# A trunk of six modulated sub-layers on one core: its opening in two parts of 512 features, with the modulation's sums in PSUM and two issuing queues

## The chip, the cores and the metric

One core of a Trainium2 chip runs the whole program, once per execution. The metric is the device time of one execution in microseconds (us), the median of three. Shorter is better.

## What is computed

The reference takes 256 rows of 1024 features through two layers of three sub-layers each. Every sub-layer computes, with `cs = silu(c)`,

```python
mod = (cs @ mod_w[layer] + mod_b[layer]).reshape(bsz, N_SUB, 3, D_MODEL)
shift, scale, gate = m[:, None, 0], m[:, None, 1], m[:, None, 2]
y = f(x * (1 + scale) + shift)
return layer_norm(DEEPNORM_ALPHA * x + (1 + gate) * y, ln_g, ln_b)
```

For the first, third, fourth and sixth sub-layer `f` is a SwiGLU, `0.5 * (silu(u @ w_gate) * (u @ w_up)) @ w_down`, with 2816 inner features; the second is a sparse attention beside a gated DeltaNet, the fifth a latent attention. All data are float32. `mod_w` has 1024 rows and, for each sub-layer, three parts of 1024 columns: shift (part 0), scale (part 1) and gate (part 2).

## The kernel before

Features lie on the 128 partitions, so a vector of 1024 features is 8 columns of 128. A product in near float32 precision is made of three TensorE passes: each operand is split into a rounded high part (ScalarE, the CAST of line 258) and the rest (the subtraction of line 259, on VectorE or GpSimd, called "low part" here). `u`, the modulated input, is kept as `uT`, features by rows, in both parts.

The modulation vectors come from `mod_gen` (line 185). It loads `mod_w` in pieces of 128 rows, and VectorE adds `w * c_k` into a 128x1024 sum in SBUF, one SCALAR_TENSOR_TENSOR per piece (line 225; the first of a sum is the TENSOR_SCALAR of line 218). TensorE then adds over the partitions: with matmuls against a column of ones for the first sub-layer (`mod_cols0`, line 142, matmul at 147), with a matmul against a matrix of ones for a gate (`mod_gate`, lines 180 and 182). `mod_gen` is a Python generator; `pace` draws from it while the SwiGLU runs, so that the eight gate rows of the first sub-layer are summed during its chunks.

The opening is everything up to the first SwiGLU product. All loads go through SyncE's queue: the four scale DMAs and the first three of shift (two pieces each, 1 MB, rows of 4 KB; the tag `w8` has three buffers), with `x` behind the scale, then the last two pieces of shift and the first two column blocks of gate and up weights. VectorE sums all 1024 features of scale, then of shift. `make_u` (line 269) with both row blocks turns `x` into `acc` banks (line 282), applies scale and shift to 256 features at a time (lines 296 on VectorE and 298 on ScalarE) and splits the result. The SwiGLU then walks 11 chunks of 256 inner features: `load` (line 439) fetches 1 MB of gate and 1 MB of up weights, TensorE makes 96 products of 128x256 (chunk 0 in the order of the list at line 495, line 540; the others through `mm3`, lines 263 to 265), and each chunk is followed by the down products of the chunk before (24 of 128x512, `down`, with weights from `load_down`, line 456). Down weights share three buffers of the tag `wd` with the gate rows of `mod_w`; the low part of the first eight down tiles is made on GpSimd.

`setup_rest` hands out small set-up work (masks, positions) between chunks. The order on each engine is set by a list scheduler that has its own cost model; `behind(...)` only forces one instruction after another on its engine. SyncE's queue issues in order: a DMA that waits, for a free buffer or for an earlier DMA on the same one of eight completion lanes (DMAHW0 to DMAHW7), holds all that stand behind it.

`warm` issues an idle TensorE product; nothing reads it.

## Time and profile before

| | us |
|---|---|
| median of 3 runs | 1210.27 (1207.26 to 1211.66) |
| the profiled execution | 1209.47 |
| its span, first to last instruction | 1207.7 |
| first SwiGLU product starts | 31.93 |
| last of chunk 1's gate and up products done, first down product | 58.02 |

Times of day below count from the span's start. The span is 1.8 us shorter than the execution that it comes from, and that execution is 0.8 us below the median. A timeline row gives start and length, the engine, the line of the kernel, the operation, and what it writes and reads (output<-inputs); in brackets is the idle time before it and what ended that. Matmul lengths overlap each other, so the distance between starts tells more than a length. A buffer's number is left out of names.

### The profile page before, as it was taken

To read this page: it belongs to the slowest core of one execution; us is meant where nothing else is said; L and a number is where in the kernel's file an instruction comes from. 1 tells how busy PE (TensorE), PEld (TensorE's weight loads), DVE (VectorE), ACT (ScalarE), POOL (GpSimd) and SP (SyncE) were. 2 spreads that over 40 slices of the span, in tenths; PEclk is the share of its full clock that TensorE was granted. 3 is DMA by queue.
4 is the path that set the end of the run, shared out by engine and by line. 5 is a ranking of instruction groups with operands and counts; after the bars stand their busy time and mean duration, and the time that the engine had idled before them with its cause. 6 is when DMAs were issued, how large, how long until landed. Compare 5 with 4: busy or idle time off the path is not lost.

```text
span 1207.7 us, 19560 instructions
## 1 busy us (share of the span) xinstructions
PE 1131.0 (94%) x7703; PEld 1025.9 (85%) x7703; DVE 917.7 (76%) x1404; ACT 548.5 (45%) x963; POOL 259.4 (21%) x186
## 2 busy tenths in 40 slices
PE   4998999998899998999999999999989998999997
PEld 3887999788787887989999899898988877899995
DVE  6699777698986677878775889767789748866545
ACT  0645444456433445543543543434347656544430
POOL 0631000224731452320000342000122234300001
PEclk9998999999999999999999899999989999999999
DMA  9879998453310576789987488888733335885620
GB/s 354 266 252 342 299 327 299 139 179 119 97 36 5 188 270 218 238 293 320 311 298 248 134 284 283 270 278 298 250 122 102 139 105 190 294 253 185 211 71 35
DMA packets 155333, 259.74 MB, mean 215 GB/s; under 512 B 8813, under 2 KB 117354, under 8 KB 155242
## 3 DMA queue, kind: packets, MB, share of 16 engines
q1 hardware_dynamic: 155050, 258.45, 64.4%
q8 instruction: 60, 0.98, 0.3%
q14 instruction: 31, 0.25, 0.1%
q10 hardware_dynamic: 192, 0.05, 0.0%
HBM read 257.43 MB, written 1.05 MB: 214 GB/s over the span
## 4 chain that ended last, share of the span: by engine, by line
PE 51%; DVE 23%; DMA 13%; issue 5%; ACT 4%; POOL 3%; SPq 0%; POOLq 0%; DVEq 0%; ACTq 0%
PE gu L265 8%; PE gu L263 8%; PE gu L264 8%; PE acc L265 6%; PE acc L264 6%; PE acc L263 6%; DMA wd<-ffn_w_down 5%; DMA wd<-mod_w 4%; DVE macc L225 3%; DMA w<-ffn_w_up 2%; DVE g L259 2%; DVE x L383 1%; POOL hd L259 1%; DMA w<-mod_w 1%; DVE u L259 1%
## 5 line engine op out<-in xcount | busy, mean ns | idle before, releaser
L225 DVE SCALAR_TENSOR_TENSOR macc<-wd,csT,macc 128x1024 f32<-128x1024 f32 x112 | 171.5, 1531 | 28.6 <-DMA wd<-mod_w 28.0
L265 PE MATMUL gu<-uT,g 128*128 128x256 f32 x640 | 181.3, 283 | 1.6 <-DVE g L259 1.6
L263 PE MATMUL gu<-uT,g 128*128 128x256 f32 x640 | 181.2, 283 | 1.3 <-ACT sg L548 1.3
L265 PE MATMUL gu<-uT,u 128*128 128x256 f32 x640 | 181.3, 283 | 1.0 <-DVE u L259 1.0
L263 PE MATMUL gu<-uT,u 128*128 128x256 f32 x640 | 181.2, 283 | 0.0
L264 PE MATMUL gu<-uT,u 128*128 128x256 f32 x640 | 181.1, 283 | 0.0
L264 PE MATMUL gu<-uT,g 128*128 128x256 f32 x640 | 181.1, 283 | 0.0
L258 ACT CAST hd<-wd 128x1024 fp32r<-128x1024 f32 x88 | 92.3, 1049 | 136.8 <-DMA wd<-ffn_w_down 118.8
L263 PE MATMUL acc<-hd,h 128*128 128x512 f32 x352 | 141.5, 402 | 0.5 <-ACT h L258 0.5
L265 PE MATMUL acc<-hd,h 128*128 128x512 f32 x352 | 138.0, 392 | 1.8 <-DVE h L259 1.8
L264 PE MATMUL acc<-hd,h 128*128 128x512 f32 x352 | 138.1, 392 | 0.0
L259 DVE TENSOR_TENSOR g<-w,g 128x1024 fp32r<-128x1024 f32 x86 | 117.0, 1364 | 23.9 <-ACT g L258 23.8
L263 PEld LDWEIGHTS gu<-uT,g 128*128 128x128 f32 x640 | 122.7, 192 | 3.2 <-ACT sg L548 1.8
L265 PEld LDWEIGHTS gu<-uT,g 128*128 128x128 f32 x640 | 122.7, 192 | 2.2 <-DVE g L259 2.2
L264 PEld LDWEIGHTS gu<-uT,g 128*128 128x128 f32 x640 | 122.7, 192 | 1.4
L265 PEld LDWEIGHTS gu<-uT,u 128*128 128x128 f32 x640 | 122.9, 192 | 1.2 <-DVE u L259 1.2
L264 PEld LDWEIGHTS gu<-uT,u 128*128 128x128 f32 x640 | 122.9, 192 | 0.0
L263 PEld LDWEIGHTS gu<-uT,u 128*128 128x128 f32 x640 | 122.9, 192 | 0.0
L259 DVE TENSOR_TENSOR u<-w,u 128x1024 fp32r<-128x1024 f32 x81 | 106.6, 1321 | 20.1 <-ACT u L258 20.0
L259 POOL TENSOR_TENSOR hd<-wd,hd 128x1024 fp32r<-128x1024 f32 x32 | 89.6, 2806 | 137.9 <-ACT hd L258 137.9
L258 ACT CAST u<-w 128x1024 fp32r<-128x1024 f32 (+1 forms) x89 | 91.7, 1038 | 58.1 <-DMA w<-ffn_w_up 44.8
L259 POOL TENSOR_TENSOR hl<-w,hl 128x1024 fp32r<-128x1024 f32 x28 | 72.5, 2602 | 202.0 <-ACT hl L258 201.5
(403 smaller groups left out, 2477.6 us busy)
## 6 DMA issues: line engine op xcount, KB each, us to landing
wd<-mod_w SPq DMA_DIRECT2D x130, 512.0 KB, 4.8
wd<-ffn_w_down SPq DMA_DIRECT2D x88, 512.0 KB, 4.6
w<-ffn_w_gate SPq DMA_DIRECT2D x43, 1024.0 KB, 8.4
w<-ffn_w_up SPq DMA_DIRECT2D x43, 1024.0 KB, 6.3
w<-hyb_w_in SPq DMA_DIRECT2D x16, 1024.0 KB, 6.1
w<-mod_w SPq DMA_DIRECT2D x7, 1024.0 KB, 7.5
w<-hyb_w_out SPq DMA_DIRECT2D x4, 1024.0 KB, 5.0
w<-mla_w_out SPq DMA_DIRECT2D x4, 1024.0 KB, 5.1
```

The lines of the kernel that those rows point to most:

```text
L225: step = nc.vector.scalar_tensor_tensor(acc, w, c, acc, ALU.mult, ALU.add)
L258: i = self.nc.scalar.copy(hi, src)
L259: return i, (eng or self.nc.vector).tensor_tensor(out=lo, in0=src, in1=hi.bitcast(F32), op=ALU.subtract)
L263: nc.tensor.matmul(out, lh, rh, start=first, stop=False)
L264: nc.tensor.matmul(out, lh, rl, start=False, stop=False)
L265: self.last_mm = nc.tensor.matmul(out, ll, rh, start=False, stop=last)
L383: V.tensor_tensor(out=x[:, b, sl], in0=tmp, in1=x[:, b, sl], op=ALU.add)
```

## The change

The first sub-layer's scale and shift leave `mod_gen`; `opening`, called from `ffn`, makes them in two halves of 512 features. For each half `open` loads scale (two pieces of 128x4x512, rows of 2 KB), then shift, and adds them in a PSUM bank; only the last addition writes SBUF. `x` comes in two halves and the first half (features 0 to 511) of the weights of chunks 0 and 1 with it, issued by ScalarE (`early`, `load(c, 0)`); the second half of these weights goes through SyncE. GpSimd makes the low parts of six of the eight weight pieces (128x1024 each), VectorE of two. TensorE makes chunk 0's products of the first half (48), then, after the second half's scale is summed over partitions and `x` is turned, chunk 1's (48), and then the second halves of both. One `warm` call of six idle products follows the first turn of `x`, one of two stands ahead of the second halves.

```diff
+    def open(self, hf, after, first, second):
+
+
+        nc, t = self.nc, self.t
+        cols, ks = slice(hf * 512, hf * 512 + 512), slice(4 * hf, 4 * hf + 4)
+        A, B = self.AB[0]
+        for i in (1, 0):
+            acc, pt = self.open_acc[i][:, cols], self.bank("gu")
+            for q in range(2):
+                if i and not q:
+                    first()
+                r = self.tl(self.wp, [P, 4, 512], "w8", bufs=3)
+                src = t["mod_w"][0, q * 512 : (q + 1) * 512, i * D + hf * 512 : i * D + hf * 512 + 512]
+                nc.sync.dma_start(r, src.rearrange("(q p) f -> p q f", p=P))
+                for k in range(4):
+                    c = self.cs[:, 4 * q + k : 4 * q + k + 1]
+                    if q or k:
+                        nc.vector.scalar_tensor_tensor(acc if q and k == 3 else pt, r[:, k], c, pt, ALU.mult, ALU.add)
+                    else:
+                        nc.vector.tensor_scalar_mul(pt, r[:, k], c)
+            if not i:
+                second()
+            pt = pt[:, 0:4]
+            with self.behind(*after):
+                for k in range(4):
+                    nc.tensor.matmul(pt[:, k : k + 1], acc[:, k * P : (k + 1) * P], self.one[:, 0:1], start=True, stop=True)
+            if i:
+                nc.vector.scalar_tensor_tensor(A[:, ks], pt, 1.0, self.bcol[:, 0, 1, ks], ALU.add, ALU.add)
+                turned = []
+                for k0 in range(4 * hf, 4 * hf + 4, 2):
+                    px = self.bank("acc", (P, 2, S))
+                    turned.append((k0, px))
+                    with self.behind(*after):
+                        for q in range(2):
+                            for b in range(NB):
+                                nc.tensor.transpose(px[:, q, b * P : (b + 1) * P],
+                                                    self.x[:, b, (k0 + q) * P : (k0 + q + 1) * P], self.ident)
+                if not hf:
+                    self.warm(self.x[:, 0, 0:512], 6)
             else:
...
+                nc.vector.tensor_tensor(out=B[:, ks], in0=pt, in1=self.bcol[:, 0, 0, ks], op=ALU.add)
+        for k0, px in turned:
+            v = self.tl(self.wp, [P, 2, S], "tmp", bufs=2)
+            nc.vector.tensor_scalar(v[:, 0], px[:, 0], A[:, k0 : k0 + 1], B[:, k0 : k0 + 1], ALU.mult, ALU.add)
+            nc.scalar.activation(v[:, 1], px[:, 1], AF.Identity, scale=A[:, k0 + 1 : k0 + 2], bias=B[:, k0 + 1 : k0 + 2])
+            self.marks[1:] = self.split(self.u[:, 0, k0 : k0 + 2], self.u[:, 1, k0 : k0 + 2], v)
...
+    def opening(self, wg, wu, gp):
+
+
+        nc, t = self.nc, self.t
+        self.x = self.tl(self.wp, [P, NB, D], "x")
+        self.open_acc = [self.tl(self.wp, [P, D], "G", bufs=2) for _ in range(2)]
+        self.AB[0] = [self.tl(self.const, [P, KD], n, bufs=3) for n in "AB"]
+        self.u = u = self.tl(self.wp, [P, 2, KD, S], "uT", F32R)
+        hls, pts, seen = {}, {}, []
+
+        def load(c, hf):
+            if hf:
+                both = self.tl(self.wp, [P, 2, 4, 256], "w8", bufs=3)
+            for g, w in enumerate((wg, wu)):
+                r = both[:, g] if hf else self.tl(self.wp, [P, 4, 256], "wd", bufs=3)
+                src = w[hf * 512 : hf * 512 + 512, c * 256 : (c + 1) * 256]
+                (nc.sync if hf else nc.scalar).dma_start(r, src.rearrange("(k p) f -> p k f", p=P))
+                hls[c, hf, g] = hl = self.tl(gp, [P, 2, 4, 256], "gu"[g], F32R)
+                seen[:] = self.split(hl[:, 0], hl[:, 1], r, None if hf and not g else nc.gpsimd)[:1]
+
+        def early(hf):
+            cols = slice(hf * 512, hf * 512 + 512)
+            with self.behind(*seen):
+                nc.scalar.dma_start(self.x[:, :, cols], t["x"][0][:, cols].rearrange("(b p) d -> p b d", p=P))
+            with self.behind(*seen):
+                load(hf, 0)
+
+        def products(c, hf):
+            if not hf:
+                pts[c] = [self.bank("gu" if c else "acc", (P, 2, S)) for _ in range(2)]
+            for kp in (0, 2):
+                for q in range(3):
+                    for s in range(2):
+                        for g in range(2):
+                            for k in (kp, kp + 1):
+                                self.last_mm = nc.tensor.matmul(
+                                    pts[c][s][:, g], hls[c, hf, g][:, q // 2, k, s * P : (s + 1) * P], u[:, q % 2, 4 * hf + k],
+                                    start=not (hf or k or q or g), stop=hf == 1 and q == 2 and k == 3, skip_group_check=True)
+
+        self.setup_bias()
+        self.open(0, (), lambda: early(0), lambda: None)
+        products(0, 0)
+        self.open(1, (self.last_mm,), lambda: early(1), lambda: [load(0, 1), load(1, 1)])
+        products(1, 0)
+        with self.behind(self.last_mm):
+            self.warm(self.x[:, 0, 0:512], 2)
+
+        def rest(c):
+            products(c, 1)
+            return {(s, g): pts[c][s][:, g] for s in range(2) for g in range(2)}
+
+        return rest
```

In `mod_gen` the list begins with the gate, and `ffn` and `run` take the new path:

```diff
-        todo = [(si, i, k) for si in range(len(self.subs)) for i in (1, 0, 2) for k in range(KD)]
-        ws, loaded, G, step = {}, 0, None, None
+        todo = [(si, i, k) for si in range(len(self.subs)) for i in (1, 0, 2) for k in range(KD) if si or i == 2]
+        ws, loaded, G = {}, 0, None
...
-                        yield
+                ahead = None
+                part = self.opening(wg, wu, gp)
...
             for c in range(NC):
                 tok = c == 0 and ahead is not None
                 with self.behind(*self.marks if c == 1 and ahead else hm.get(c - 2, ())):
-                    if c or ahead:
+                    if c > 1 or ahead:
                         hls = ahead if tok else load(c, False)
                 if tok:
                     rows = by_rows(hls)
                 else:
-                    pts = {(s, g): self.bank("gu", (P, S)) for s in r2 for g in r2}
-                    if c:
+                    if c < 2 and not ahead:
+                        pts = part(c)
+                    else:
+                        pts = {(s, g): self.bank("gu", (P, S)) for s in r2 for g in r2}
...
-        self.lead = 0
+        self.lead, self.count = 0, 2 * KD
+        self.AB, self.G, self.mdone = {}, {}, {(0, 0), (0, 1)}
...
-        self.need(0, 1)
-        self.count += next(self.bg)
-        todo = self.todo = [self.sublayer(si, l, j) for si, (l, j) in enumerate(subs)]
-        self.make_u(0, self.x, range(NB))
+        todo = [self.sublayer(si, l, j) for si, (l, j) in enumerate(subs)]
```

`warm` issues `n` products into one bank, and `mod_cols0`, `load_x`, the joint branch of `make_u` and the interleaving order of chunk 0 are gone.

How the instructions now stand, at three places. Names end in a buffer number; what is in square brackets is what the instruction waits for.

**SyncE's queue at the start.** `w` is a piece of the modulation weights, `prow` the small parameter loads of the set-up, `wd` a down weight tile. Before:

```order
L202 DMA w_5_82<-mod_w 128x2x1024
L202 DMA w_6_86<-mod_w 128x2x1024
L202 DMA w_7_90<-mod_w 128x2x1024 [waits DMAHW1_49]
L202 DMA w_8_94<-mod_w 128x2x1024 [waits DMAHW2_49,DVE_49]
L325 DMA x_118<-x 128x2x1024 [waits DMAHW3_49]
L202 DMA w_14_121<-mod_w 128x2x1024 [waits DMAHW4_49,DVE_49]
L202 DMA w_22_149<-mod_w 128x2x1024 [waits DMAHW5_49,DMAHW1_49,DVE_49]
L202 DMA w_23_153<-mod_w 128x2x1024 [waits DMAHW6_49,DMAHW2_49,DVE_49]
```

Now:

```order
L266 DMA w_19_116<-mod_w 128x4x512
L266 DMA w_20_122<-mod_w 128x4x512
L266 DMA w_25_151<-mod_w 128x4x512
L100 DMA prow<-ln_g 48x128 [waits DMAHW5_49,DVE_49]
L101 DMA prow<-ln_b 48x128 [waits DMAHW6_49]
L102 DMA prow<-mla_q_norm_g 3x128 [waits DMAHW7_49]
L103 DMA prow<-mla_kv_norm_g 2x128 [waits DMAHW1_49]
L483 DMA wd_420<-ffn_w_down 128x1024 [waits DMAHW4_49,Pool_49]
L266 DMA w_26_157<-mod_w 128x4x512 [waits DMAHW5_49,DMAHW2_49,DVE_49]
L266 DMA w_36_240<-mod_w 128x4x512 [waits DMAHW6_49,DVE_49]
L266 DMA w_37_246<-mod_w 128x4x512 [waits DMAHW7_49,DVE_49]
```

Of the eight modulation pieces three are issued at once. The fourth (w_26, the second piece of the first half's shift) stands behind `prow`, whose third load waits on lane 7, that of w_25, and behind down tile 0 (wd_420), which waits for GpSimd: its buffer is the one that chunk 0's first up piece leaves when its low part is made.

**VectorE at the start, now.** gu_104 is the bank of the scale's sum, gu_150 that of the shift's, both of the first half.

```order
L81 COPY csT<-gu_77 128x8 [waits PE_49]
L272 TENSOR_SCALAR gu_104<-w_19_116,csT 128x512 [waits DMAHW2_49,DVE_49]
L272 TENSOR_SCALAR gu_150<-w_25_151,csT 128x512 [waits DMAHW7_49]
L270 SCALAR_TENSOR_TENSOR gu_104<-w_19_116,csT,gu_104 128x512 [waits DVE_49]
L270 SCALAR_TENSOR_TENSOR gu_150<-w_25_151,csT,gu_150 128x512 [waits DVE_49]
```

The alternation goes on through the four 128x512 parts of w_19 and of w_25, then come the four of w_20, and the four of w_26 behind them. So the second addition of scale stands behind the first of shift, which waits for w_25 (lane 7). Before, one sum was finished before the other began.

**SyncE's queue in the first chunks.** `G` rows are the gate's rows of `mod_w` (line 182 now, 198 before). Before:

```order
L458 DMA wd_489<-ffn_w_down 128x1024 [waits DVE_49]
L458 DMA wd_500<-ffn_w_down 128x1024 [waits DMAHW5_49,DMAHW2_49,Pool_49]
L212 DMA G_506<-mod_b 128x1024
L198 DMA wd_508<-mod_w 128x1024 [waits DMAHW6_49,DMAHW4_49,Pool_49]
L198 DMA wd_511<-mod_w 128x1024 [waits DMAHW1_49,Pool_49]
```

Now:

```order
L467 DMA w_80_559<-ffn_w_gate 128x8x256 [waits DMAHW1_49,DVE_49]
L467 DMA w_81_560<-ffn_w_up 128x8x256 [waits DMAHW4_49,DMAHW2_49,DMAHW5_49,DVE_49,Pool_49]
L483 DMA wd_503<-ffn_w_down 128x1024 [waits DMAHW3_49,Pool_49]
L182 DMA wd_511<-mod_w 128x1024 [waits Pool_49]
L182 DMA wd_514<-mod_w 128x1024 [waits Pool_49]
L467 DMA w_102_782<-ffn_w_gate 128x8x256 [waits DMAHW7_49,DMAHW6_49,DVE_49]
L483 DMA wd_681<-ffn_w_down 128x1024 [waits DMAHW3_49,Pool_49]
```

Before, down tiles 2 and 3 and the first gate row went out ahead of chunk 2's weights; now chunk 2's weights are ahead, and down tile 3 (wd_503) and the first two gate rows each wait for GpSimd to finish a down tile's low part.

## Rows read from the trace of the kernel before

**Rows 1.** The page, busy time of TensorE, share of the span, instructions.
```profile
PE 1131.0 (94%) x7703; PEld 1025.9 (85%) x7703; DVE 917.7 (76%) x1404; ACT 548.5 (45%) x963; POOL 259.4 (21%) x186
```

**Rows 2.** Stages of the span, TensorE: length, busy (records), granted clock, DMA share, GB/s.
```profile
32.00:44.00 12.00, 12.00 (x94) 1.00 0.90 292
44.00:58.00 14.00, 12.81 (x105) 1.00 0.64 223
58.00:93.00 35.00, 33.62 (x237) 1.00 0.78 262
93.00:103.00 10.00, 5.82 (x16) 0.66 1.04 358
103.00:230.00 127.00, 127.00 (x887) 1.00 0.85 287
```

**Rows 3.** Timeline of TensorE, 46 to 104 us: start, length, operation, idle before.
```profile
46.61 0.39 PE L265 MATMUL gu<-uT,g 128*128 128x256 f32 x1 [1.19 <-DVE g L259]
...
58.02 0.48 PE L265 MATMUL acc<-hd,h 128*128 128x512 f32 x1
...
97.92 3.75 PE L180 MATMUL gu<-macc,one 128*128 128x512 f32 x4 [4.18 <-DVE macc L225]
100.69 1.41 PE L263 MATMUL acc<-hd,h 128*128 128x512 f32 x1
...
102.98 0.39 PE L264 MATMUL acc<-hd,h 128*128 128x512 f32 x1
```

**Rows 4.** Waits of TensorE from 32 to 230 us: total, times, longest.
```profile
PE gu L180 <- DVE macc L225: 4.2, 1, 4.2
```

**Rows 5.** One line of TensorE by its source: ns min/median/max of one.
```profile
L180 PE MATMUL gu<-macc,one x24: 590/592/1191, 97.9 to 1184.6; 128*128 128x512 f32 x24
```

**Rows 6.** The DMA view of 0 to 45 us: GB/s in 40 equal slices.
```profile
GB/s 0 11 153 408 415 418 412 383 408 390 390 426 411 411 419 408 408 411 408 419 404 415 411 329 291 289 290 290 290 329 401 394 353 349 213 22 110 365 378 387
```

**Rows 7.** Timeline of VectorE in the opening, the same columns.
```profile
6.22 0.75 DVE L218 TENSOR_SCALAR G<-w,csT 128x1024 f32<-128x1024 f32 x1 [3.19 <-DMA w<-mod_w]
...
9.05 7.91 DVE L225 SCALAR_TENSOR_TENSOR G<-w,csT,G 128x1024 f32<-128x1024 f32 x6 [0.76 <-DMA w<-mod_w]
```

**Rows 8.** Groups by form, the down weights on ScalarE and GpSimd.
```profile
L258 ACT CAST hd<-wd 128x1024 fp32r<-128x1024 f32 x88 | 92.3, 1049 | 136.8 <-DMA wd<-ffn_w_down 118.8 <-PE acc L265 10.9 <-POOL poscr L622 6.8
...
L259 POOL TENSOR_TENSOR hd<-wd,hd 128x1024 fp32r<-128x1024 f32 x32 | 89.6, 2806 | 137.9 <-ACT hd L258 137.9
```

**Rows 9.** Groups by form, VectorE: shapes, count, busy us, mean ns, idle before.
```profile
L225 DVE SCALAR_TENSOR_TENSOR macc<-wd,csT,macc 128x1024 f32<-128x1024 f32 x112 | 171.5, 1531 | 28.6 <-DMA wd<-mod_w 28.0
...
L381 DVE SCALAR_TENSOR_TENSOR tmp<-acc,G 128x512 f32<-128x512 f32 x18 | 12.0, 678 | 6.8 <-PE acc L265 6.8
```

**Rows 10.** Timeline of TensorE in the opening, the same columns.
```profile
26.71 1.96 PE L124 MATMUL gu<-x,ident 128*128 128x512 f32 x4
28.75 1.92 PE L147 MATMUL gu<-one,G 128*128 128x1 f32 x16
...
31.93 0.80 PE L540 MATMUL gu<-uT,g 128*128 128x256 f32 x2
```

**Rows 11.** Timeline of ScalarE in the opening.
```profile
30.52 0.56 ACT L298 ACTIVATE tmp<-acc,B,A 128x256 f32<-128x256 f32 x1 [0.46 <-DVE B L168]
31.12 0.62 ACT L258 CAST uT<-tmp 128x512 fp32r<-128x512 f32 x1
```

**Rows 12.** DMA issues by line: KB each, median us to landing.
```profile
wd<-mod_w SPq DMA_DIRECT2D x130, 512.0 KB, 4.8
```

**Rows 13.** Timeline of VectorE, the position operations and the last gate row.
```profile
90.99 0.28 DVE L618 TENSOR_SCALAR posc<-posi 128x258 int32<-128x258 int32 x1
...
96.50 1.28 DVE L225 SCALAR_TENSOR_TENSOR macc<-wd,csT,macc 128x1024 f32<-128x1024 f32 x1
```

**Rows 14.** Timeline of GpSimd and of VectorE around 78 us.
```profile
77.16 3.04 POOL L259 TENSOR_TENSOR hd<-wd,hd 128x1024 fp32r<-128x1024 f32 x1 [6.99 <-ACT hd L258]
...
77.87 3.42 DVE L225 SCALAR_TENSOR_TENSOR macc<-wd,csT,macc 128x1024 f32<-128x1024 f32 x1
```

More of the change, by code (lines that the diff above doesn't have):

```diff
@@ L239, in mod_sums @@
         elif i == 1:
-            if si:
-                self.mod_scale(si, self.mod_cols(acc))
-            else:
-                self.scale = self.mod_cols0(acc, self.one[:, 0:1])
-        else:
-            if not si:
-                with self.behind(step):
-                    self.mod_scale(si, self.scale)
-                    self.nc.vector.tensor_tensor(out=self.AB[0][1], in0=self.share[:, 0:KD], in1=self.bcol[:, 0, 0],
-                                                 op=ALU.add)
+            self.mod_scale(si, self.mod_cols(acc))
+        else:
             self.mod_shift(si, acc)
@@ L301, in make_u @@
-        if joint:
-            pts = [rows(k0) for k0 in range(0, KD, 2)]
-            vs = self.tl(self.wp, [P, 2, 2, W], "macc")
-            self.warm(n[:, 0, 0:512])
-            while self.count < 2 * KD:
-                self.count += next(self.bg)
-            next(self.todo[0])
-            self.need(si, 0)
-            with self.behind(self.last_col):
-                for _ in range(2):
-                    self.warm(n[:, 0, 0:512])
-            for k0 in range(0, KD, 2):
-                with self.behind(self.marks[1]):
-                    affine(k0, pts[k0 // 2])
-                if k0 < 4:
-                    with self.behind(self.marks[1]):
-                        self.marks[1:] = self.between[k0 // 2]()
-        else:
-            for k0 in range(0, KD, 2):
-                affine(k0, rows(k0))
@@ L558, in ffn @@
                         load_down(i)
-                    with self.behind(*[part] if c == 1 else after):
+                    with self.behind(*[made] if c == 1 else after):
                         self.pace(max(0, i + 1 - skip) / (NT - 2 - skip))
@@ L562, in ffn @@
                 if c > 1 and self.left is not None:
-                    with self.behind(part):
+                    with self.behind(made):
                         next(self.left, None)
```

135 lines of the change are left out of this document (32 added, 103 removed).

## The prediction

> **What bounds the kernel now.** I read the page first: TensorE is busy 1131.0 us, 94% of the span [rows 1]. So I looked for the stretches in which it is not, and cut the span into stages [rows 2]. From 103 to 230 us it has 127.00 us of records in 127: whatever delay reaches that stage comes out at the end one for one, since every engine's order is the old one from there on. Lost time lies ahead of it: all of 0 to 31.93, 1.19 in the stage 44 to 58 [rows 3], 1.38 (35.00 - 33.62) in 58 to 93, and 4.18 before the gate's product at line 180 (97.92), which waited for the last gate row's sum (TensorE's waits, [rows 4]). In that last stage the granted clock is 0.66, in all others 1.00. The 1.19 us wait at 46.61 left its stage at 1.00; the 4.18 did not.
>
> What the 4.18 cost besides itself: from 97.92 to 102.98 stand four records of line 180 and four 128x512 products [rows 3]. The products took 2.29 us; at twice the 0.128 us of a 128x256 product (12.00 / 94, [rows 2]) they take about 1.0. The four took 2.77; their median length elsewhere is 0.592 against 0.94 (3.75 / 4), [rows 5], so about 1.0 of it is lost too. I take 2.4 (1.3 if only the products are counted).
>
> The opening, 0 to 31.93, is bounded by loads: from 3.4 us on the DMA view shows 383 to 426 GB/s in nearly all slices, some 290 where the 512-byte rows of the first weight columns run, 350 to 400 where shapes mix [rows 6]. VectorE starts when the first 1 MB is in, at 6.22, and goes on waiting for loads [rows 7].
>
> **The change, part by part.**
>
> *Loads ahead of the first product.* Before, 8 MB of modulation; now 4 MB of it, half of x and 0.5 MB each of gate and up for chunk 0. That 5.5 MB would take 14.3 us at 385 GB/s (my value for 1 and 2 KB rows, between 290 and 411). The queues don't let it: only three modulation pieces have buffers. Issue order gives, from 2.8 us on (2.6 us for each MB, and 0.8 from last byte to use): x 5.0, w_19 7.7, gate 9.0, w_20 11.8, w_25 14.5, up 15.9. VectorE's second addition of scale waits for w_25; the sum of w_19 and w_20 is then about 14.5 + 9 x 0.72 = 21 us, and w_26 wants w_19's buffer, free around 19.
>
> *The fourth piece.* w_26 stands besides behind down tile 0, which waits for GpSimd's low part of chunk 0's up. Up lands at 15.9, its cast takes 1.05, the low part 2.81 [rows 8]: 19.8, so w_26 goes out at about 20.3. By then the rest of what ScalarE issued, and the down tile, are ahead of it: some 3.1 MB from 18.5 us on, so it lands at 27.5. Four additions follow.
>
> *Additions in PSUM.* No row of before writes a sum of two to PSUM. The nearest is line 381, 128x512 with one PSUM source, 0.678 us; the SBUF sums are 7.91 / 6 = 1.32 for 1024 [rows 7, 9]. Bounds are 0.66 (half of 1.32) and 1.32 (half the columns save nothing). I take 0.72: the shape is that of line 381. The count is unchanged in columns, 16 x 1024, so nothing hinges on it except the last four: 27.5 + 4 x 0.72 = 30.4.
>
> *From the last sum to the first product.* One 0.5 us addition of the next half gets in ahead; four column sums on TensorE 0.5 to 1.0 (16 in 1.92, [rows 10]); then addition of the bias, the scaling 0.54 on VectorE beside 0.56 on ScalarE, and the cast 0.62 [rows 11], with hand-overs: 4.2 us. First product at **34.6**, against 31.93 [rows 10]. With 411 GB/s, both sums early and no extra addition, 31.0; with 350 GB/s, 36.5.
>
> *Chunks 0 and 1.* 48 products of the first half are 48 x 0.128 = 6.1, plus 2.4 for a cold clock after the long wait: 43.2. Column sums and eight turns of x, 0.9 each by [rows 10]: 45.0. Chunk 1's 48 and the shift's columns: 52.0. The idle products are four records, 2.0 (1.96 at 26.71): 54.0. The 96 of the second halves 12.3: **66.3**. Before, that point was 58.02 [rows 3]. So TensorE is 8.3 us late there. The second half's 4 MB of modulation follows w_26 and lands by 38.4 at 385 GB/s; the second weight halves, 2 MB, by 45. Neither is late for its products.
>
> *The gate.* The work from there to line 180 took 35.7 us with 1.38 of waits (58.02 to 93.72). Without those it comes to L180 at 66.3 + 34.3 = 100.6, against 97.92. Whether it waits there depends on column row 7 of the gate. SyncE's queue now has chunk 2's weights ahead of down tile 3 and the gate, and each gate row takes a buffer that GpSimd gives up. One round is a 0.5 MB load of 4.8 [rows 12], a cast of 1.05 and a low part of 2.81 [rows 8]: 8.7 us. Down tile 3's load waits for tile 0's low part, tile 4's for tile 3's, tile 5's for tile 4's, and gate row 5 for tile 5's. I put tile 0's at 60.4, as it stands behind those of the weights; then tile 3's at 69.1, tile 4's at 77.8, tile 5's at 86.5. Gate row 5 lands at 91.3, rows 6 and 7 behind it. The position operations ahead of the last addition take 5.5 us (90.99 to 96.50, [rows 13]) and I let them end at 99.4, when the rows are in. The last addition ends about 100.7, and L180 starts at about **101.0**.
>
> So the wait shrinks from 4.18 to some 0.5 us, under the 1.19 that left the clock at 1.00, and the 2.4 comes back.
>
> *Sum.* L180 starts 101.0 - 97.92 = 3.1 later; 2.4 is given back by the warm clock: **+0.7**. The rest of the program carries it unchanged. On the profiled execution's 1209.47 (0.8 under the median of 1210.27) that is 1210.2 us. Removed work besides (the interleaving list, the fewer bank changes) I put at nothing: it lay beside loads.
>
> *A page against the row.* The DMA view gives one rate for the whole core, not who gets it. My arrival times assume order of issue across the two queues. The Trainium skill ("DMA: Bandwidth & Descriptors", section "Queues, rings and completion order") says that each DMA engine takes turns between the queues that have work. By that rule up would land at an estimated 14.4 rather than 15.9, and the sum would be 0.7 lower, if all the rest stays; no row here shows two busy queues.
>
> **The rivals.**
>
> *The opening is shorter than I say and nobody waits at line 180* (faster). Loads run at 411 GB/s, POOL's part is done early, the first product comes at 31.0. Its first half is not cold, as the idle products run up to it, and the second half begins with no gap: 31.0 + 6.1 + 1.8 + 7.0 + 2.0 + 12.3 = 60.2. L180 is reached at 94.5 and, if the gate's rows are in by then, not waited for. That is 3.4 earlier, and 2.4 for the clock: -5.8, **1203.7 us**. For it: the opening's DMA share is full, so any byte saved counts. Against it: the three buffers and down tile 0 ahead of w_26, and the gate's rounds of 8.7 us.
>
> *The gate's last row becomes the bound* (slower). Two VectorE sums with both sources in SBUF coincide with GpSimd low parts. In before one such pair shows it: GpSimd 77.16 for 3.04, VectorE 77.87 for 3.42 where 1.28 is usual [rows 13, 14]: 2.14 lost. With every gate row behind a low part, two more such pairs put the last row at 105.3; TensorE, there at 100.6, waits 4.7 us and the clock falls as before. That is 105.3 - 97.92 = **+7.4, 1216.9 us**. It decides once L180 starts after about 104, for then the wait is near the 4.18 that cost the clock. The Trainium skill ("SBUF — State Buffer", section "Who interferes with whom") has an exclusive lock between VectorE and GpSimd for this; the 3.42 agrees.
>
> *The change does not do what it says.* In my forecast that is so already: the half opening gives no earlier product, since the fourth piece waits.
>
> **How the numbers follow.** The forecast's case, within a few us of L180 at 101, gets 0.6; the faster rival 0.2; the slower 0.2. Around the forecast the first product's bounds (31.0 to 36.5) give -3.6 to +1.9, and the last four PSUM additions at 1.32 another +2.4. An interval from 1203.5 to 1217.0 takes in both rivals. A measurement of this kernel tells 0.5%, 6.05 us, from no change: faster is below 1204.2, slower above 1216.3. The faster rival passes that in most of its cases, 0.16, plus 0.02 of the others: **0.18**. The slower one in most of its, 0.16, plus 0.02: **0.18**. Same: **0.64**.
>
> **What would show it.** Right: the first product at 33 to 36 us, VectorE idle before its first shift addition and again before w_26's; down 0 at 64 to 68; L180 at about 101 after a wait under 1.2 us, with granted clock near 1.00 in 93 to 105. Wrong: a first product before 28 us (the queue's hold is not real), a wait over 2 us inside chunks 0 and 1 (the second half's modulation or weights come late), or a wait over 4 at line 180 with a clock under 0.8.

## The result, and the profile after

The changed kernel takes **1217.89 us** (median of 4 runs, 1216.23 to 1219.77), the kernel before 1209.32 in the same comparison (4 runs, 1207.26 to 1211.66): a ratio of 1.0071, 95% interval 1.0045 to 1.0096. It is slower, by 0.9 us more than the range's upper end. The profiled execution took 1217.08 with a span of 1215.3.

The stages of TensorE, as in [rows 2] (length, busy with records, granted clock, DMA share, GB/s):

```profile
32.00:44.00 12.00, 9.08 (x56) 0.64 0.80 280
44.00:58.00 14.00, 14.00 (x109) 1.00 0.96 312
58.00:93.00 35.00, 34.34 (x244) 1.00 0.72 232
93.00:103.00 10.00, 7.71 (x65) 1.00 0.77 236
103.00:230.00 127.00, 121.83 (x850) 0.97 0.91 303
```

Its timeline at the points of [rows 3] and [rows 10]: first product, first down product, gate. In brackets is the idle time before and what ended it.

```profile
36.19 0.80 PE L417 MATMUL acc<-uT,g 128*128 128x256 f32 x2 [2.92 <-ACT uT L221]
...
66.47 0.49 PE L226 MATMUL acc<-hd,h 128*128 128x512 f32 x1
...
108.17 3.75 PE L166 MATMUL gu<-macc,one 128*128 128x512 f32 x4 [7.45 <-DVE macc L199]
110.93 1.42 PE L226 MATMUL acc<-hd,h 128*128 128x512 f32 x1
```

TensorE stands ready for the gate (line 166 now) at 108.17 - 7.45 = 100.7, against 97.92 - 4.18 = 93.7 before. So it arrives 7.0 us later and then waits 3.3 us longer; line 166 starts 10.25 later. As before, the clock is low after the wait: the granted clock of 108 to 112 is 0.50, the lower of the two levels (1.2 GHz), and from 108.17 to 110.93 the four records take 2.76 us, 2.77 before.

GpSimd's timeline in the same profile; its `hd` rows are the low parts of down tiles:

```profile
25.46 2.33 POOL L222 TENSOR_TENSOR u<-wd,u 128x1024 fp32r<-128x1024 f32 x1
51.73 2.37 POOL L222 TENSOR_TENSOR u<-w,u 128x1024 fp32r<-128x1024 f32 x1 [23.93 <-ACT u L221]
54.59 3.47 POOL L222 TENSOR_TENSOR u<-w,u 128x1024 fp32r<-128x1024 f32 x1 [0.49 <-ACT u L221]
58.00 10.35 POOL L222 TENSOR_TENSOR hd<-wd,hd 128x1024 fp32r<-128x1024 f32 x4
...
75.41 3.70 POOL L222 TENSOR_TENSOR hd<-wd,hd 128x1024 fp32r<-128x1024 f32 x1 [6.67 <-ACT hd L221]
86.43 6.49 POOL L222 TENSOR_TENSOR hd<-wd,hd 128x1024 fp32r<-128x1024 f32 x1 [7.32 <-ACT hd L221]
```

SyncE's queue there, the same view (DMA issues: start, length, line, what is loaded; `posi` are the rows that VectorE's position operations read):

```profile
63.28 2.88 SPq L182 DMA_DIRECT2D wd<-mod_w  x2
...
79.14 0.33 SPq L483 DMA_DIRECT2D wd<-ffn_w_down  x1
...
92.95 1.60 SPq L182 DMA_DIRECT2D wd<-mod_w  x2
94.60 0.42 SPq L614 DMA_DIRECT2D posi<-positions  x1
95.08 0.43 SPq L615 DMA_DIRECT2D posi<-positions  x1
...
99.10 1.97 SPq L182 DMA_DIRECT2D wd<-mod_w  x2
```

GpSimd is idle from 27.8 to 51.7, then makes the second halves' low parts, and only at 58.00 the first four down tiles'. The gate's rows go out from 63.28 on (the first two), from 92.95 (the sixth and seventh) and at 99.10 (the eighth); before, the first went out at 45.5. The end of VectorE's sum, its timeline there:

```profile
89.43 1.21 DVE L222 TENSOR_TENSOR u<-w,u 128x1024 fp32r<-128x1024 f32 x1
90.56 0.41 DVE L550 TENSOR_TENSOR sg<-gu,sg 128x256 f32<-128x256 f32 x1
90.90 3.10 DVE L605 TENSOR_SCALAR mI<-mge 128x128 f32<-128x128 f32 x1
92.92 1.27 DVE L199 SCALAR_TENSOR_TENSOR macc<-wd,csT,macc 128x1024 f32<-128x1024 f32 x1
...
99.43 1.28 DVE L199 SCALAR_TENSOR_TENSOR macc<-wd,csT,macc 128x1024 f32<-128x1024 f32 x1 [0.36 <-DMA wd<-mod_w]
100.65 0.30 DVE L617 TENSOR_SCALAR posc<-posi 128x258 int32<-128x258 int32 x1
...
106.74 1.28 DVE L199 SCALAR_TENSOR_TENSOR macc<-wd,csT,macc 128x1024 f32<-128x1024 f32 x1
```

The eighth row's addition stands behind the position operations (100.65 to 106.74), whose loads went out behind the sixth and seventh row.

Behind 108.17 the order is the old one. At the end of the first sub-layer the program is 9.9 us late, at that of the third 10.2, at that of the fourth 7.6, and so to the end. The 2.7 come out of the fourth sub-layer. There TensorE waits 5.3 us in all for modulation sums (line 138) in the profile of before and 4.2 (line 139 now) in this one; that is 1.1 of the 2.7, and the rest is open.

### The profile page after: what moved, and what is told of

It is laid out like the page before. It is cut to its first block, busy times and chain, and to the rows that moved or that the text cites. A ratio compares the mean times of both kernels' runs of the same rounds, so it can differ in the third digit from the quotient of the medians.

```text
span 1215.3 us, 19553 instructions
## 1 busy us (share of the span) xinstructions
PE 1132.5 (93%) x7693; PEld 1025.9 (84%) x7693; DVE 918.3 (76%) x1416; ACT 546.9 (45%) x961; POOL 265.1 (22%) x187
## 3 DMA queue, kind: packets, MB, share of 16 engines
HBM read 257.43 MB, written 1.05 MB: 213 GB/s over the span
## 4 chain that ended last, share of the span: by engine, by line
PE 53%; DVE 25%; DMA 11%; ACT 4%; issue 4%; POOL 2%; SPq 0%; DVEq 0%; POOLq 0%; ACTq 0%
PE gu L228 8%; PE gu L226 8%; PE gu L227 8%; PE acc L228 6%; PE acc L226 6%; PE acc L227 6%; DMA wd<-mod_w 4%; DMA wd<-ffn_w_down 3%; DVE macc L199 3%; DVE g L222 3%; DMA w<-ffn_w_up 2%; DMA w<-mod_w 2%; DVE u L222 1%; DVE x L355 1%; PE gu L769 1%
## 5 line engine op out<-in xcount | busy, mean ns | idle before, releaser
L199 DVE SCALAR_TENSOR_TENSOR macc<-wd,csT,macc 128x1024 f32<-128x1024 f32 x112 | 161.4, 1441 | 32.7 <-DMA wd<-mod_w 32.2
L226 PE MATMUL gu<-uT,g 128*128 128x256 f32 x624 | 176.6, 283 | 1.5 <-ACT sg L547 1.5
L226 PE MATMUL gu<-uT,u 128*128 128x256 f32 x624 | 176.6, 283 | 0.0
L227 PE MATMUL gu<-uT,u 128*128 128x256 f32 x624 | 176.6, 283 | 0.0
L228 PE MATMUL gu<-uT,g 128*128 128x256 f32 x624 | 176.6, 283 | 0.0
L228 PE MATMUL gu<-uT,u 128*128 128x256 f32 x624 | 176.6, 283 | 0.0
L227 PE MATMUL gu<-uT,g 128*128 128x256 f32 x624 | 176.6, 283 | 0.0
L221 ACT CAST hd<-wd 128x1024 fp32r<-128x1024 f32 x88 | 91.9, 1049 | 123.0 <-DMA wd<-ffn_w_down 108.2
L222 DVE TENSOR_TENSOR g<-w,g 128x1024 fp32r<-128x1024 f32 x86 | 120.5, 1403 | 17.7 <-ACT g L221 17.7
L221 ACT CAST u<-w 128x1024 fp32r<-128x1024 f32 x86 | 89.7, 1048 | 76.3 <-DMA w<-ffn_w_up 64.5
L226 PEld LDWEIGHTS gu<-uT,g 128*128 128x128 f32 x624 | 119.6, 192 | 3.3 <-ACT sg L547 1.9
L222 DVE TENSOR_TENSOR u<-w,u 128x1024 fp32r<-128x1024 f32 x78 | 99.0, 1274 | 30.2 <-ACT u L221 30.1
L227 PEld LDWEIGHTS gu<-uT,g 128*128 128x128 f32 x624 | 119.6, 192 | 1.4
L226 PEld LDWEIGHTS gu<-uT,u 128*128 128x128 f32 x624 | 119.8, 192 | 0.0
L227 PEld LDWEIGHTS gu<-uT,u 128*128 128x128 f32 x624 | 119.8, 192 | 0.0
L228 PEld LDWEIGHTS gu<-uT,u 128*128 128x128 f32 x624 | 119.8, 192 | 0.0
L228 PEld LDWEIGHTS gu<-uT,g 128*128 128x128 f32 x624 | 119.6, 192 | 0.0
```

What stands on the lines that cost most here:

```text
L199: nc.vector.scalar_tensor_tensor(acc, w, c, acc, ALU.mult, ALU.add)
L221: i = self.nc.scalar.copy(hi, src)
L222: return i, (eng or self.nc.vector).tensor_tensor(out=lo, in0=src, in1=hi.bitcast(F32), op=ALU.subtract)
L226: nc.tensor.matmul(out, lh, rh, start=first, stop=False)
L227: nc.tensor.matmul(out, lh, rl, start=False, stop=False)
L228: self.last_mm = nc.tensor.matmul(out, ll, rh, start=False, stop=last)
```

## The experiments

Two theories stood against each other at first. **G**: the end is set by the chain of the gate's rows, which hangs on the down tiles' buffers. **O**: it is set by the later opening. **Q**, the rival to both, takes the queue as a whole for the bound: what one load gains another loses. The table gives, for each kernel's profile, when TensorE was ready for the gate's matmuls, when they started, and the measured ratio to the kernel before, with its interval. A profile is of one execution, and some lie off their medians: those of down_dve_first (1207.7 us) and order_nowarm_bias (1208.1) some 4 us under, those of onb_row and row_first some 3 over, that of onb_early 3.0 under. So differences of 2 us between a gate's start and a median tell nothing.

| kernel | ready | gate's start | us, median | ratio |
|---|---|---|---|---|
| before | 93.7 | 97.9 | 1209.3 | 1 |
| the change | 100.7 | 108.2 | 1217.9 | 1.0071 (1.0045 to 1.0096) |
| no_warm | 99.9 | 107.7 | 1218.3 | 1.0081 (1.0062 to 1.0101) |
| row_first | 101.6 | 107.9 | 1219.2 | 1.0097 (1.0078 to 1.0115) |
| order | 100.4 | 106.8 | 1217.4 | 1.0077 (1.0060 to 1.0094) |
| order_nowarm | 99.9 | 106.5 | 1216.0 | 1.0063 (1.0043 to 1.0082) |
| early_down | 100.9 | 103.0 | 1213.4 | 1.0033 (1.0017 to 1.0048) |
| early_down_pos | 99.9 | 101.1 | 1212.4 | 1.0035 (1.0019 to 1.0052) |
| order_nowarm_bias | 95.1 | 101.9 | 1212.0 | 1.0031 (1.0016 to 1.0046) |
| onb_row | 95.7 | 100.0 | 1209.8 | 1.0022 (1.0007 to 1.0036) |
| onb_early | 99.9 | 103.3 | 1215.3 | 1.0064 (1.0042 to 1.0086) |
| down_dve_first | 99.7 | 101.0 | 1211.8 | 1.0025 (1.0007 to 1.0043) |
| down_dve | 102.2 | 102.7 | 1200.8 | 0.9935 (0.9916 to 0.9954) |
| onb_down_dve | 94.8 | 95.8 | 1195.3 | 0.9888 (0.9871 to 0.9906) |
| before_down_dve | 91.4 | 94.4 | 1196.3 | 0.9888 (0.9869 to 0.9906) |
| late_gate | 106.8 | 108.8 | 1219.7 | 1.0085 (1.0063 to 1.0107) |
| before_late_gate | no wait | 98.9 | 1208.6 | 1.0000 (0.9986 to 1.0014) |
| order_nowarm_early | no wait | 108.7 | 1218.3 | 1.0080 (1.0061 to 1.0098) |
| order_nowarm_early_pos | 108.0 | 108.1 | 1217.2 | 1.0071 (1.0055 to 1.0087) |

**The chain of the gate.** In `early_down` tiles 0 and 1 need not wait for `u`:

```diff
-                    with self.behind(*after):
+                    with self.behind(*(after if ahead else ())):
                         load_down(i)
```

> Theory G (the gate's chain): the loss is the 7.45 us that TensorE waits at line 166 for the gate's last row, and that row is late because the low parts of down tiles 0 to 2 are made at 58 us, behind the split of u's second half. Without that order tile 0's low part is made before 40 us, the first gate row goes out near 45 us instead of 63.3, line 166 starts at or before 103, and the time is 1208 to 1213. Rival Q (the queue as a whole is the bound): gate rows that go out earlier push chunk 2's weights back, TensorE waits in chunk 2 instead, and the time stays within 2 us of 1217.9. Rival O (the late opening): the first product and chunk 2's start don't change, so the time doesn't either.

GpSimd's timeline in it:

```profile
27.89 2.35 POOL L222 TENSOR_TENSOR hd<-wd,hd 128x1024 fp32r<-128x1024 f32 x1
43.76 4.75 POOL L222 TENSOR_TENSOR hd<-wd,hd 128x1024 fp32r<-128x1024 f32 x2 [13.53 <-ACT hd L221]
```

TensorE's, at the gate:

```profile
103.03 1.96 PE L166 MATMUL gu<-macc,one 128*128 128x512 f32 x4 [2.14 <-DVE macc L199]
```

Tile 0's low part runs at 27.89 and the first gate row goes out at 46.2. TensorE is ready at 100.9, as before the edit, the gate starts 5.1 us earlier, and 4.5 us are won (1213.39). Ready time alone, theory O, would have left the time where it was. G's forecast holds here.

`late_gate` leaves the chain as it is and takes TensorE's two matmul calls out of the way:

```diff
+        while self.count < goal and not self.pending:
...
+            with self.behind(*[self.last_mm][si:]): nc.tensor.matmul(pt, self.one, acc[:, h * 512 : (h + 1) * 512], start=True, stop=True)
...
+            self.pending = (si, acc, G) if (si, i) == (0, 2) else self.mod_sums(si, i, acc, G)
...
+                if self.pending: self.pending = self.mod_gate(*self.pending)
...
```

> Only the gate's two matmul calls are moved behind the 24 products of down tiles 4 and 5. Theory G: these products fill 5.5 us of the 7.45 us wait and the clock stays up, so 1217.9 falls by 5 to 8, to 1210 to 1213. Rival Q: chunk 4's up weights, which go out at 101 us and are split at 112, are the next wait; TensorE waits there for about what it won, and the time is 1215 to 1218.

> The kernel before with the gate's two matmul calls behind the products of down tiles 4 and 5. Theory G: the 4.18 us wait and the 2.4 us of a low clock go: 1209.3 falls to 1203 to 1205. Rival Q: chunk 4's weights, out at 91.5 us, are the next wait, at about 99 us: 1206 to 1208.

Neither gave anything: 1219.73 and 1208.63. G's forecast missed in both. In the kernel before the 4.18 us wait and the low clock did go and the first sub-layer ended 4.4 us earlier, but by the end of the fourth it was 0.5 late. In the changed kernel the wait fell from 7.45 to 2.04 us and the first sub-layer ended 1.5 us earlier, but the third ended 1.5 later and the fourth 3.8 later. The edit changes the order of everything behind it, so this says only that a wait taken out of one sub-layer can come back in others; why it came back isn't settled. What the gate's chain costs can't be read from TensorE's wait alone.

`row_first` changes VectorE's order alone: position operations (line 617 and on) and chunk 4's low parts behind the last gate row.

```diff
+                self.row = nc.vector.scalar_tensor_tensor(acc, w, c, acc, ALU.mult, ALU.add)
...
+                with self.behind(*[self.row] if not ahead and c == 3 else []): next(self.rest, None)
...
+                with self.behind(*self.marks if c == 1 and ahead else hm.get(c - 2, ()), *[self.row] if c == 4 and not ahead else []):
```

> The changed kernel; on VectorE alone the gate's last row is summed ahead of the position operations and of chunk 4's low parts (6.1 us of work that stood ahead of it: 100.65 to 106.74). The queue is untouched, so the row lands when it did. It went out at 99.1; with 4.8 us to landing it is in at 104 and summed at 105.3. Theory G (the end follows the start of line 166): line 166 starts at 105.0 to 106.0 instead of 108.2, the time falls by 2 to 3, to 1215 to 1216. Rival (what VectorE leaves behind is then late for chunk 4, and TensorE waits there): line 166 is earlier and the time is still 1217 to 1219.

VectorE's timeline in it:

```profile
101.23 1.29 DVE L199 SCALAR_TENSOR_TENSOR macc<-wd,csT,macc 128x1024 f32<-128x1024 f32 x1 [2.40 <-DMA wd<-mod_w]
104.45 3.27 DVE L199 SCALAR_TENSOR_TENSOR macc<-wd,csT,macc 128x1024 f32<-128x1024 f32 x1 [1.93 <-DMA wd<-mod_w]
107.65 0.28 DVE L617 TENSOR_SCALAR posc<-posi 128x258 int32<-128x258 int32 x1
```

And GpSimd's:

```profile
104.30 2.35 POOL L222 TENSOR_TENSOR hd<-wd,hd 128x1024 fp32r<-128x1024 f32 x1 [1.31 <-ACT hd L221]
```

A miss, and the most telling run. The row landed at 104.4, VectorE stood idle for it for 1.93 us, and then its addition took 3.27 us instead of 1.28, for GpSimd had begun a low part at 104.30. Taking the 6.1 us of position work out of the way won only 0.3 us at the gate. In the change the trace has the row in at 103.05, and its addition waited for the position work until 106.74; here the row was in 1.3 us later, and the collision took 2.0 more. So GpSimd keeps the row late, on the way to its load and here in the sum itself. Where the row is early, the position work does count. In `early_down_pos` (the first two lines of that edit, on early_down) the gate starts 1.9 us earlier than in early_down, and the time moves by less than the intervals tell.

> As early_down, with the position operations on VectorE behind the gate's last row instead of ahead of it. Theory G: line 166 starts as soon as that row is in, 100.9 to 101.5 instead of 103.0, with less than 0.7 us of wait; 1.5 to 2 us less than early_down. Rival (the row itself lands only at 101.6): no change.

**GpSimd out of the chain.** `down_dve` gives the low parts of the first eight down tiles to VectorE, in all four SwiGLUs; `down_dve_first` in the first sub-layer alone; `before_down_dve` is the same edit on the kernel before.

```diff
-                self.split(dl[:, 0], dl[:, 1], r, nc.gpsimd if i < 8 else None)
+                self.split(dl[:, 0], dl[:, 1], r, None)
```

> The changed kernel with the low parts of the first eight down tiles on VectorE (1.2 us each) instead of GpSimd (2.4 to 6.5 us each, and 2 us more for a VectorE operation that meets one). The order on the queue is the same as far as the gate's sixth row. Theory P (a gate row goes out only when GpSimd has given back one of three buffers, so GpSimd's part sets the chain): the rows go out earlier, line 166 starts at 102 to 105 instead of 108.2, and the time is 1212 to 1215. Rival (the buffers are held by loads and casts, or VectorE is full): line 166 at 107 or later, 1216 to 1220.

> down_dve set GpSimd aside in all four SwiGLUs and came out 17 us under the changed kernel, 7.4 of it by the end of the first sub-layer and another 7.7 in the fourth. Here it is set aside in the first sub-layer alone, where the change was made. Theory P: line 166 at 102 to 103 as in down_dve, the first sub-layer 7 us earlier, the fourth unchanged; 1209 to 1212. Rival (the gain of the fourth sub-layer is a shift of phase that the first brings with it): 1200 to 1203.

> The kernel before with the low parts of the first eight down tiles on VectorE in all four SwiGLUs. Theory P: its gate rows also hang on GpSimd, less so (first row out at 45.5): line 180 goes from 97.9 to 94 to 96 and the clock stays up, some 5 us; the fourth sub-layer gives 6 to 8 as there; 1195 to 1199, as fast as onb_down_dve or less than 3 us behind it. Rival (GpSimd's chain is new with the change and the kernel before loses nothing by it): only the fourth sub-layer's part, 1200 to 1203.

Busy time by engine on the page of the change, then on that of `down_dve`:

```profile
PE 1132.5 (93%) x7693; PEld 1025.9 (84%) x7693; DVE 918.3 (76%) x1416; ACT 546.9 (45%) x961; POOL 265.1 (22%) x187
```

```profile
PE 1127.4 (94%) x7693; PEld 1023.1 (85%) x7693; DVE 907.8 (76%) x1448; ACT 549.1 (46%) x961; POOL 177.3 (15%) x155
```

Three groups of VectorE (count | busy us, mean ns | idle before): its gate additions, the low parts of gate weights (`g`) and of the inner features (`h`). The change first, `down_dve` behind it:

```profile
L199 DVE SCALAR_TENSOR_TENSOR macc<-wd,csT,macc 128x1024 f32<-128x1024 f32 x112 | 161.4, 1441 | 32.7 <-DMA wd<-mod_w 32.2
L222 DVE TENSOR_TENSOR g<-w,g 128x1024 fp32r<-128x1024 f32 x86 | 120.5, 1403 | 17.7 <-ACT g L221 17.7
...
L222 DVE TENSOR_TENSOR h<-sg,h 128x256 fp32r<-128x256 f32 x82 | 44.0, 539 | 12.0 <-ACT h L221 12.0
```

```profile
L199 DVE SCALAR_TENSOR_TENSOR macc<-wd,csT,macc 128x1024 f32<-128x1024 f32 x112 | 148.6, 1327 | 20.7 <-DMA wd<-mod_w 19.9 <-DVE macc L199 0.4
L222 DVE TENSOR_TENSOR g<-w,g 128x1024 fp32r<-128x1024 f32 x86 | 107.7, 1252 | 19.4 <-ACT g L221 19.1
...
L222 DVE TENSOR_TENSOR h<-sg,h 128x256 fp32r<-128x256 f32 x82 | 34.3, 420 | 10.9 <-ACT h L221 10.7
```

The gate in TensorE's timeline of `down_dve`, then of `before_down_dve`:

```profile
102.71 1.96 PE L166 MATMUL gu<-macc,one 128*128 128x512 f32 x4 [0.51 <-DVE macc L199]
```

```profile
94.36 3.35 PE L180 MATMUL gu<-macc,one 128*128 128x512 f32 x4 [2.98 <-DVE macc L225]
```

In the first sub-layer alone the edit is worth 6.1 us (1211.78 against 1217.89): line 166 starts at 101.0 after 1.2 us of wait. In all four it is worth 17.1, and 12.3 to the kernel before. VectorE takes over 32 operations of 1.2 us, 37.5 us more of low parts of down tiles, and is still busy 10.5 us *less* (907.8 against 918.3). Its gate additions lose 12.8 us, the low parts of gate weights 12.8 and those of `h` 9.7, at the same counts; the other 12.7 lie in smaller pieces. The mean of a gate addition falls from 1441 to 1327 ns.

**The opening.** `order` puts the sum of scale ahead of that of shift, and the set-up's loads and down tile 0 behind the modulation on the queue.

```diff
+                self.held = nc.sync.dma_start(r, src.rearrange("(q p) f -> p q f", p=P))
...
+                        with self.behind(*gate): nc.vector.tensor_scalar_mul(pt, r[:, k], c)
...
+                with self.behind(*[] if ahead else [self.held]): nc.sync.dma_start(r, wd[i * P : (i + 1) * P, :])
...
+            with self.behind(self.held): self.setup_params()
```

(`gate` is the last addition of scale.)

> The sum of scale ahead of that of shift on VectorE, and the fourth piece of modulation no longer behind the set-up's loads and down tile 0. Both theories: first product at 25 to 28 us instead of 36.2. Theory G: down tile 0's low part still stands behind the second half of u, so the gate's chain moves by about as much as u does (5 to 8 us); line 166 starts near 101 to 103 after a wait of some 5 us; 1209 to 1213. Rival O (the opening alone sets the end): the wait at line 166 goes and the time falls by the whole 9 us or more, to 1206 to 1209. Rival Q: no change, since the queue is the bound from 40 us on: 1216 to 1219.

First product at 36.36: nothing won. VectorE waited 7.37 us for the scale's columns, which stand behind the twelve records of idle products on TensorE (17.5 to 24.0). Without those (`order_nowarm`) it was still 35.86, for the fourth piece went out only at 16.97, and took 8.5 us beside x's second half and chunk 1's weights. What held it back shows in the waits of SyncE's queue in order_nowarm (total, times, longest):

```profile
SPq L266 <- DMA w<-mod_w: 17.0, 2, 13.8
```

It waited 13.8 us for a piece of the modulation. The trace has the fourth piece on the completion lane of the third, which VectorE first reads at 16.90. The expectation of order_nowarm_bias, below, puts the wait down to the last of six 8 KB bias loads; that one landed at 17.04, after the piece had gone out. What the six do, as I read it, is take up lanes, so that the fourth piece comes to the third's. `order_nowarm_bias` makes those loads two:

```diff
-                if not hf:
-                    self.warm(self.x[:, 0, 0:512], 6)
...
-        for si, (l, j) in enumerate(self.subs):
-            src = t["mod_b"][l, 3 * j * D : (3 * j + 2) * D].rearrange("(r p) -> r p", p=P)
-            nc.scalar.dma_start(rows[si * n : (si + 1) * n], src)
+        for l in range(2):
+            src = t["mod_b"][l].rearrange("(j r p) -> j r p", j=3, p=P)[:, 0:n]
+            nc.scalar.dma_start(rows[l * 3 * n : (l + 1) * 3 * n], src)
```

> As in order, and without the six idle products that stood ahead of the scale's column sums on TensorE (in order VectorE waited 7.37 us for those columns, behind the idle products). First product at 26 to 29 us instead of 36.2, chunk 2 reached about 8 us earlier. Theory G (the end is set by the gate's chain, which hangs on u's second half through down tiles 0 and 1): tile 0's low part comes 5 to 8 us earlier and line 166 starts at 100 to 103; 1208 to 1212. Rival O (the late opening sets the end): the whole 8 us is won, 1208 to 1210, and no wait at line 166 is left. Rival Q (the queue is the bound from 40 us on): line 166 starts no earlier than 106; 1216 to 1219.

> order_nowarm with the six small bias loads on ScalarE's queue made two. In order_nowarm the fourth modulation piece went out only at 16.97 us, when the last of the six had landed, and landed at 25.48. Now it waits for VectorE alone: out near 12.7, landed by 19 to 20, first product at 24 to 28 us. Theory O (the late opening is worth the 7 us by which TensorE reaches line 166 later, 100.7 against 93.7): with the first product 8 us earlier TensorE gets there at 92 to 94. Theory G: line 166 itself still waits for the last gate row, to 100 or later, and the time is 1209 to 1213, about 5 less than order_nowarm. Rival Q: line 166 stays at 106 and the time at 1215 to 1218.

TensorE's timeline in order_nowarm_bias, the first product and the gate:

```profile
31.04 0.79 PE L415 MATMUL acc<-uT,g 128*128 128x256 f32 x2 [2.97 <-ACT uT L221]
...
101.92 3.37 PE L166 MATMUL gu<-macc,one 128*128 128x512 f32 x4 [6.79 <-DVE macc L199]
```

Now the piece has another lane, that of chunk 0's first gate piece, and goes out at 12.63. The first product is at 31.04, 5.2 us earlier than in the change (24 to 28 were expected: VectorE has the last sum only at 26.1). TensorE is ready 5.6 earlier, and still waits 6.79 us for the gate, as G has it. The gate's chain came forward with the opening, since tile 0's low part still stands behind the second half of `u`; so the opening counts here through the chain.

The warming products alone:

> The changed kernel without the six idle products alone. They end at 25.66 us, 5.7 us ahead of the shift's column sums, and the granted clock of 32 to 44 us is 0.64 with them. Theory: they neither help the clock nor hold anything (scale's columns come 1 us earlier, the fourth piece lands at 28.2 as before): first product at 36 us, time within 1.5 us of 1217.9. Rival (they are what keeps the first products from being slower still): the first 48 products take longer than the 7.75 us they take now and the time rises by 1 to 3.

1218.25, no difference. The pairs of products start 0.43 us apart at first either way, and 0.24 later: ending 10 us ahead of the first product, the idle products warm nothing here.

**Both together.** `order_nowarm_early` and `order_nowarm_early_pos` (order_nowarm with early_down, and with the position edit) came to 1218.34 and 1217.19, `onb_early` (order_nowarm_bias with both edits) to 1215.28.

> order_nowarm and early_down together. Theory G: the opening's 8 us and the gate's chain come forward together; TensorE reaches line 166 near 93 and starts it at 96 to 99; 1204 to 1208, at or under the kernel before. Rival Q: line 166 starts at 103 as in early_down, after a wait of about 10 us; 1212 to 1214.

> order_nowarm_early with the position operations behind the gate's last row. Theory G: another 2 to 4 us off line 166's wait; 1202 to 1206. Rival Q: the last row is bound by the queue, and the time equals that of order_nowarm_early within 1 us.

> order_nowarm_bias, with down tiles 0 and 1 no longer behind u's second half and the position operations behind the last gate row. Theory G: both the opening and the gate's chain are early; line 166 starts at 95 to 99; 1203 to 1208. Rival Q: as in order_nowarm_early, chunk 3's up weights are then late (TensorE waited 4.27 us for them there), line 166 starts at 104 or later and the time is 1212 to 1218.

Here Q was right: with the gate's first rows ahead of chunk 2's and 3's weights these come late (4.27 us of wait at 97.90 in order_nowarm_early), and the gate starts at 103 to 109 all the same. `onb_row` is order_nowarm_bias with row_first's edit, `onb_down_dve` that with down_dve's:

> order_nowarm_bias with the same edit. There TensorE stood ready at 95.1 and line 166 started at 101.92; the row went out at about 91.4 and 9 us of other work on VectorE (91.28 to 100.50) stood ahead of it. Theory G: line 166 starts at 96.5 to 98, after a wait of 1.4 to 3 us, and the time falls by 3 to 5 from 1211.96, to 1207 to 1209, level with the kernel before. Rival: chunk 4's low parts are late instead, and the time stays at 1211 to 1213.

> onb_row with the same edit. Theory P: line 166 at 95.5 to 98, wait under 2.5 us; 1205 to 1208, level with or under the kernel before. Rival: VectorE's added 9.6 us (8 x 1.2) delay low parts of the weights, and TensorE waits there; 1209 to 1213.

onb_row is 2.2 us under order_nowarm_bias by the medians, 1.1 by the ratios, whose intervals overlap: not settled. With GpSimd out too the gate starts at 95.8 after 1.0 us, and **1195.34 us** (0.9888) beats the change and the kernel before; it equals before_down_dve (1196.34, the same ratio). What beats both is the edit to the down tiles; the opening in two parts, mended, costs and brings nothing beside it that the intervals show.

## Why the prediction was wrong

- *What bounds the kernel*: right for this change up to the third sub-layer. From line 166 on the delay carries (+10.25 there, +9.9 and +10.2 behind it). Not right to the end: 2.7 us came back in the fourth, and in before_late_gate 4.4 us won by the end of the first sub-layer were gone by then. "One for one" was too strong.
- *Loads, additions in PSUM*: right in the sum, not in every term. An addition of 128x512 takes 0.70 us from start to start (9 in 6.28), 0.72 was put. w_25 was in at 16.96 (14.5 put), and up's cast began at 14.96 (15.9 put). So the loads of two queues did not come in order of issue; the prediction's other estimate for up, 14.4 with the queues taking turns, was the nearer. w_26 went out at 21.03 (20.3 put), the first product came at 36.19 (34.6 put, 36.5 the bound).
- *Chunks 0 and 1*: right within 0.2 us, in part by luck. First down product 66.47, 66.3 put. The first product was 1.6 us later than put, and the way from there 1.4 shorter (30.3 for 31.7), most of it in the cold first products (granted clock 0.64 in 32 to 44): 7.75 us where 8.6 was put. TensorE reached line 166 at 100.7, 100.6 put.
- *The gate*: **this step failed.** "I put tile 0's low part at 60.4 ... tile 3's at 69.1, tile 4's at 77.8, tile 5's at 86.5": a round of 8.7 us. Tile 0's ended at about 60.6 and the four by 68.35, as put. Tile 4's ended at 79.11, 1.3 late, but tile 5's at 92.92: 13.8 us after it, not 8.7. Of those, 6.2 are the load and the wait for the cast (out at 79.14, cast at 85.31, 4.8 put), 1.05 the cast and 6.49 the low part, for which 2.81 was put. ScalarE's timeline has what the cast stood behind:

```profile
84.99 0.41 ACT L221 CAST h<-sg 128x256 fp32r<-128x256 f32 x1 [4.77 <-DVE sg L550]
85.31 1.05 ACT L221 CAST hd<-wd 128x1024 fp32r<-128x1024 f32 x1
```

So the round that was mis-sized is that of tile 5: the low part by 3.7 us and the wait for the cast, put at nothing, by 1.4. Row 5 (the sixth) went out at 92.95 where it was to have landed at 91.3, row 7 at 99.10. The positions were loaded behind rows 5 and 6, so the position operations ended at 106.7 where I had put 99.4, and line 166 started 7.2 us later than put. The clock that I had given back, 2.4 us, stayed lost. The sign of being wrong that I had named came: a wait over 4 us (7.45) and a clock under 0.8 (0.77 in 93 to 103).
- *The slower rival* was the right case, and its mechanism held in the main: GpSimd and VectorE hold each other up on the way of the last row, the clock falls after the wait. But it put the loss on VectorE's side, two additions of 2.14 us more each; here the loss was GpSimd's (6.49 for 2.81), and the last addition took its usual 1.28. It said 105.3 and 1216.9; measured 108.2 and 1217.9. That the time came so near is luck: the gate was 2.9 us later than it said, and 2.7 came back in the fourth sub-layer. I gave it 0.2, because I left the rounds themselves free of collisions. The trace of before had several (the mean of line 225 is 1531 ns where 1.28 us is usual, [rows 9, 13]).
- *The share of the opening.* With the chain relieved in the first sub-layer alone 3.2 us remain to the kernel before (1211.78 against 1208.62). With GpSimd out everywhere, in both kernels, 4.5 remain by the medians (1200.82 against 1196.34) and 5.7 by the ratios; mending the opening of down_dve, with row_first's order, gives 5.5 (1195.34). So of the 8.6 us lost half or a little more are the opening's, which the wait at line 166 had partly hidden, and the rest the gate's chain. That is worked out from differences between kernels that differ in more than one wait.

## What to carry to other kernels

Where a row waits for buffers that another engine gives back, its time is a sum of rounds; price each with that engine beside its neighbour (3.70 and 6.49 us here), not with its mean (2.81), and count the wait for the engine between. A forecast that rests on "the wait then vanishes" needs the late side's chain walked as far as the early side's. And look whether work was put on a slower engine to spare a faster one that it then holds up: taking it back made both less busy here.

## What the hardware showed

GpSimd's 128x1024 subtraction takes 2.33 us with VectorE all but idle (25.46 in the timeline after) and 6.49 beside it (86.43). VectorE's 128x128 operation at 90.90 has a record of 3.10 us, and the next on VectorE starts only at 92.92, where GpSimd ends; the same form (line 601) takes 0.21 at 87.75. In row_first VectorE's addition took 3.27 for 1.28.

The 6.49 can be read more closely. VectorE's low part at 89.43, inside it, takes its usual 1.21. From 90.56, where VectorE turns to an operation that reads a PSUM bank, to GpSimd's end at 92.92 are 2.36 us, the length of a subtraction alone; SyncE's next gate row, which waits for that end, goes out at 92.95. So, as I read it, GpSimd waited some 4 us through several VectorE operations in a row and then ran in one piece, and VectorE waited for that in turn. No run changes this alone.

The Trainium skill ("SBUF — State Buffer", section "Who interferes with whom") has the two engines contend for an exclusive lock, which the first to start holds for its whole instruction; the 3.27 agrees (GpSimd's low part ended at 106.65; with 1.28 behind it that is 107.93, and the addition ended at 107.72). That the loss goes both ways, and is so large that VectorE is less busy with 32 operations more, is what I had not expected.
